# Hybrid decoder trunk, two layers: the state-space scan as one real scan instruction over states turned back by their phase and forward again

## The chip, the cores and the metric

The kernel runs on one core of one Trainium2 chip, in one launch. The metric is the time of a launch in microseconds on the device, as the median of three runs; lower is better. Engines are named as in the profile: PE (matrix products), DVE (VectorE), ACT (ScalarE), POOL (GpSimd), SP (which issues the DMAs).

## The reference

Two layers, 512 tokens, width 1024, all in float32. What matters here is the state-space group of each layer (S5): 32 channel groups of 16 channels drive 64 complex states each.

```python
lam = lax.complex(lam_re, lam_im)
a_bar = jnp.exp(lam * dt)
b_bar = ((a_bar - 1.0) / lam)[..., None] * b_mat
bu = jnp.einsum('bsgc,gpc->bsgp', ug.astype(jnp.complex64), b_bar)
a_elems = jnp.broadcast_to(a_bar, bu.shape)
_, states = lax.associative_scan(combine, (a_elems, bu), axis=1)   # x[s] = a_bar x[s-1] + bu[s]
y = jnp.einsum('bsgp,gcp->bsgc', states, c_mat).real.reshape(B, S, SSM_WIDTH)
```

Beside it, on the same normed input, stands an attention group of 8 heads (causal softmax in query blocks of 128). Both are normed, projected together, and added to the hidden state; then come cross-attention into 256 memory tokens and a SwiGLU feed-forward block.

## The kernel before, in words

Each matrix product is three: operands are split into a high part (ACT, L209, L238, L241) and a low part (DVE or POOL, L210, L239, L242), and `mm3` (L213) issues three matmuls. A block of weights (128x1024) is loaded by `load_w` (L203); the low parts of the memory projection's weights (`xkv`, L943) are POOL's, its result tiles in the PSUM tag `f`, which has one bank, are evicted by DVE at L959.

Tokens of the state-space group are taken eight at a time (T = 8), so that 512 tokens make 64 columns j. `s5_params` (L403) makes, once per layer, the powers of a_bar and from them the matrices by which PE turns eight inputs into a state (`s5_v`, L775), a state into eight outputs (`s5_y`, L881), and inputs into outputs directly (`s5_y0`, L864). What is left between `s5_v` and `s5_y` is the recurrence over the 64 columns with the complex factor A = a_bar^8, for 2048 states (128 partitions x 16). `s5_scan` (L800) does it in two levels: the columns as 8 x 8, seven inner steps (pieces 0 to 2, `step` at L810, six DVE instructions each on 128 to 256 elements, strided), six outer steps over the eight block ends `Sj` (piece 3, on 16 to 32 elements), and a join (pieces 4 and 5), which adds A^i times the carried state to every inner state, its real half on DVE and its imaginary half on POOL (L846 to L851). Eight DMAs (L854) bring the result into the layout `W` that `s5_y` multiplies with. Large tiles of this part share the tag `s5b`, six slots of 128x2048.

The order: attention goes in units (head, pair of query blocks), and a table `PLAN` (L164) says after which unit each part of the other work is emitted: "x" memory projection, "v" `s5_v`, "m" `s5_y0`, "c" a piece of `s5_scan`, "y", "G", "g", "s" what follows. The framework then schedules all instructions by priority, against its own timeline, and each engine's queue runs in the order that comes out. Layer 0's parameters are made at the head of the run, layer 1's during the feed-forward block of layer 0 (hook in `ffn`). A softmax (L765) is, on DVE, a reduction (L767), a reciprocal (L769) and a scaling (L773, or on ACT L771), with the exponential on ACT (L768) between.

## Time and profile before

| | |
|---|---|
| Median of 3 runs | 1632.43 us (1628.01 to 1634.59) |
| Span of the profiled execution | 1624.2 us |
| PE busy | 1517.3 us, 93% |
| DVE busy | 975.1 us, 60% |
| ACT busy | 619.6 us, 38% |
| POOL busy | 345.8 us, 21% |

The profiled execution has no time of its own besides its span; the runs' median is 8.2 us above that span. Shares over the whole span are means over stages with different limits, so the stretches in which the state-space scan runs are read by themselves: some 136 to 212 us (layer 0) and 902 to 983 us (layer 1). PEclk in the views is the granted clock of PE, as a share of the upper of its two levels.

### The profile page before, as it was taken

To read this page: it belongs to the slowest core of one execution; us is meant where nothing else is said; L and a number is where in the kernel's file an instruction comes from. 1 tells how busy PE (TensorE), PEld (TensorE's weight loads), DVE (VectorE), ACT (ScalarE), POOL (GpSimd) and SP (SyncE) were. 2 spreads that over 40 slices of the span, in tenths; PEclk is the share of its full clock that TensorE was granted. 3 is DMA by queue.
4 is the path that set the end of the run, shared out by engine and by line. 5 is a ranking of instruction groups with operands and counts; after the bars stand their busy time and mean duration, and the time that the engine had idled before them with its cause. 6 is when DMAs were issued, how large, how long until landed. Compare 5 with 4: busy or idle time off the path is not lost.

```text
span 1624.2 us, 20486 instructions
## 1 busy us (share of the span) xinstructions
PE 1517.3 (93%) x8038; PEld 1272.5 (78%) x8038; DVE 975.1 (60%) x1499; ACT 619.6 (38%) x995; POOL 345.8 (21%) x225
## 2 busy tenths in 40 slices
PE   7779798999999999999998778989999999999997
...
GB/s 224 62 130 105 85 138 135 105 91 42 127 136 99 103 96 99 89 106 91 88 156 155 133 42 146 124 118 93 75 41 92 93 102 99 96 91 105 91 90 75
DMA packets 97488, 169.09 MB, mean 104 GB/s; under 512 B 32496, under 2 KB 55536, under 8 KB 97392
## 3 DMA queue, kind: packets, MB, share of 16 engines
...
HBM read 150.00 MB, written 15.66 MB: 102 GB/s over the span
## 4 chain that ended last, share of the span: by engine, by line
PE 67%; DVE 9%; ACT 4%; DMA 2%; issue 2%; POOL 1%; SPq 1%; DVEq 0%; ACTq 0%; POOLq 0%
PE mm L216 13%; PE mm L218 13%; PE mm L217 12%; PE f L216 7%; PE f L217 7%; PE f L218 7%; ACT whi L209 1%; DVE lo L239 1%; ACT hi L238 1%; DVE s5b L927 1%; DVE wlo L210 1%; DVE sc L818 1%; PE mm L1006 1%; PE mm L1005 1%; DMA s5b<-du 1%
## 5 line engine op out<-in xcount | busy, mean ns | idle before, releaser
L209 ACT ACTIVATE whi<-wraw 128x1024 fp32r<-128x1024 f32 (+1 forms) x234 | 243.3, 1042 | 637.1 <-PE mm L217 312.3
L210 DVE TENSOR_TENSOR wlo<-wraw,whi 128x1024 fp32r<-128x1024 f32 (+2 forms) x196 | 279.4, 1426 | 68.1 <-ACT whi L209 65.9
L216 PE MATMUL mm<-hi,whi 128*128 128x512 f32 x589 | 231.3, 393 | 0.3 <-ACT whi L209 0.3
L218 PE MATMUL mm<-hi,wlo 128*128 128x512 f32 x589 | 230.0, 392 | 0.4 <-DVE wlo L210 0.4
L217 PE MATMUL mm<-lo,whi 128*128 128x512 f32 x589 | 229.7, 391 | 0.0
L1113 POOL TENSOR_TENSOR tmp<-tmp,tmp 128x512 f32<-128x512 f32 x44 | 60.4, 1374 | 573.8 <-DVE tmp L1112 518.9
L216 PE MATMUL mm<-ghi,whi 128*128 128x512 f32 (+1 forms) x368 | 147.1, 400 | 9.3 <-ACT whi L209 7.9
L218 PE MATMUL mm<-ghi,wlo 128*128 128x512 f32 (+1 forms) x368 | 146.5, 398 | 0.4 <-DVE wlo L210 0.4
L217 PE MATMUL mm<-glo,whi 128*128 128x512 f32 (+1 forms) x368 | 146.0, 398 | 0.2 <-DVE glo L239 0.2
L216 PE MATMUL f<-ghi,whi 128*128 128x256 f32 (+2 forms) x432 | 144.2, 334 | 0.0
L218 PE MATMUL f<-ghi,wlo 128*128 128x256 f32 (+2 forms) x432 | 143.0, 331 | 0.8 <-POOL wlo L210 0.8
L217 PE MATMUL f<-glo,whi 128*128 128x256 f32 (+2 forms) x432 | 142.8, 331 | 0.3 <-DVE glo L242 0.3
L216 PEld LDWEIGHTS mm<-hi,whi 128*128 128x128 f32 x589 | 110.9, 188 | 26.2 <-ACT whi L209 2.2
L218 PEld LDWEIGHTS mm<-hi,wlo 128*128 128x128 f32 x589 | 110.7, 188 | 24.5 <-DVE wlo L210 0.8
L217 PEld LDWEIGHTS mm<-lo,whi 128*128 128x128 f32 x589 | 110.8, 188 | 22.9
L210 POOL TENSOR_TENSOR wlo<-wraw,whi 128x1024 fp32r<-128x1024 f32 x38 | 92.0, 2422 | 122.0 <-ACT whi L209 97.2
L216 PE MATMUL f<-hi,whi 128*128 128x512 f32 (+1 forms) x293 | 114.6, 391 | 0.3 <-ACT whi L209 0.3
L218 PE MATMUL f<-hi,wlo 128*128 128x512 f32 (+1 forms) x293 | 114.3, 390 | 0.0
L217 PE MATMUL f<-lo,whi 128*128 128x512 f32 (+1 forms) x293 | 114.2, 390 | 0.0
L964 DVE TENSOR_TENSOR s5b<-mm,s5b 128x512 f32<-128x512 f32 x52 | 35.9, 690 | 108.2 <-PE mm L218 95.9
L238 ACT ACTIVATE hi<-tmp 128x512 fp32r<-128x512 f32 (+1 forms) x100 | 63.0, 630 | 89.4 <-POOL tmp L1113 58.9
L216 PEld LDWEIGHTS f<-ghi,whi 128*128 128x128 f32 (+1 forms) x432 | 83.0, 192 | 8.9 <-issue 0.7
...
## 6 DMA issues: line engine op xcount, KB each, us to landing
...
```

The costliest lines, as they stand in the source:

```text
L209: nc.scalar.activation(hi, raw, AF.Copy)
L210: (eng or nc.vector).tensor_tensor(lo, raw, hi.bitcast(F32), ALU.subtract)
L216: self.nc.tensor.matmul(ps, wh, xh, start=i == 0, stop=False)
L217: self.nc.tensor.matmul(ps, wh, xl, start=False, stop=False)
L218: last = self.nc.tensor.matmul(ps, wl, xh, start=False, stop=i == n - 1)
L238: a = nc.scalar.activation(hi, src, AF.Copy)
L239: b = eng.tensor_tensor(lo, src, hi.bitcast(F32), ALU.subtract)
L818: E0.tensor_tensor(t1[:, ri], src[:, ri], c(Are), ALU.mult)
L927: nc.vector.tensor_tensor(self.so[m].rearrange("p (j s) -> p s j", s=8), yS[:, m], sg.rearrange("p (s j) -> p s j", s=8), ALU.mult)
L964: self.nc.vector.tensor_tensor(self.hs[m], ps, self.hs[m], ALU.add)
L1005: self.nc.tensor.matmul(ps, hi[:, ks], xh, start=False, stop=False)
L1113: nc.gpsimd.tensor_tensor(uf, uf, gf, ALU.mult)
```

## The change

With A = |A| e^(i phi), the state of column j is turned back by j phi. Then the recurrence has the real factor |A| alone, the same for the real and the imaginary part, and one instruction, `tensor_tensor_scan`, runs it along the free dimension: state = factor x state + input. One instruction takes 8 of the 16 state groups at 64 columns, 512 elements; the factor is 0 at each group's column 0, where a new group begins. Afterwards the states are turned forward again. A half of the states (piece 0 or 1) is thus 6 products and sums on 128x8x63, two scans on 128x512 and 6 products and sums on 128x512, all on DVE, in place in `St`, and four DMAs straight from there. The imaginary half of the join on POOL goes, too.

`s5_v` writes columns 1 to 63 directly, and POOL sets column 0 to zero. `s5_params` no longer raises a_bar and A to powers by complex products (36 instructions per layer): angles are multiples, brought into range and put through the sine on ACT (432 elements for the cosine, 432 for the sine), magnitudes by three real products. A table `tab` of cosine and sine of j phi (two 128x1024) is made by ten instructions per layer and stays in an `s5b` slot until the scan is over; `rt` holds the factors. `PLAN` names two pieces "c" where there were six. The rest of the change removes comments.

```diff
...
-CID, CE, CE16, CROPE, NCONST = 0, 128, 256, 272, 276
+CID, CE, CE16, CROPE, CSTEP, NCONST = 0, 128, 256, 272, 276, 285
...
+    const[:, CSTEP:CSTEP + 9] = np.arange(9)
...
-        (-1, "x", 0), (-1, "x", 1), (1, "v", 0), (1, "m", 0), (2, "c", 0), (2, "c", 1), (2, "c", 2), (2, "x", 2),
-        (2, "m", 1), (2, "x", 3), (3, "m", 2), (3, "m", 3), (4, "c", 3), (4, "c", 4), (5, "x", 4), (7, "c", 5),
+        (-1, "x", 0), (-1, "x", 1), (1, "v", 0), (1, "m", 0), (2, "c", 0), (2, "x", 2),
+        (2, "m", 1), (2, "x", 3), (3, "m", 2), (3, "m", 3), (4, "c", 1), (5, "x", 4),
         (7, "y", 0), (8, "y", 1), (8, "y", 2), (9, "y", 3), (13, "G", 0), (13, "g", 0), (14, "x", 5), (14, "g", 1),
         (14, "g", 2), (14, "x", 6), (14, "g", 3), (15, "x", 7), (16, "s", 0),
     ), (
-        (-2, "v", 0), (-2, "c", 0), (-2, "m", 0), (0, "c", 1), (0, "c", 2), (0, "m", 1), (0, "m", 2), (0, "x", 0),
-        (0, "m", 3), (0, "x", 1), (0, "c", 3), (1, "x", 2), (2, "c", 4), (2, "c", 5), (2, "x", 3), (4, "y", 0),
+        (-2, "v", 0), (-2, "c", 0), (-2, "m", 0), (0, "c", 1), (0, "m", 1), (0, "m", 2), (0, "x", 0),
+        (0, "m", 3), (0, "x", 1), (1, "x", 2), (2, "x", 3), (4, "y", 0),
         (5, "y", 1), (6, "y", 2), (6, "y", 3), (6, "x", 4), (11, "G", 0), (12, "x", 5), (14, "g", 0), (14, "g", 1),
         (14, "g", 2), (14, "g", 3), (14, "x", 6), (16, "x", 7), (16, "s", 0),
     ))
...
-        dt, zr, zi, er = sl(), sl(), sl(), sl()
+        dt, zr, er = sl(), sl(), sl()
         P.tensor_tensor(dt, self.econst, ldt, ALU.pow)
         V.tensor_tensor(zr, lre, dt, ALU.mult)
-        V.tensor_tensor(zi, lim, dt, ALU.mult)
         P.tensor_tensor(er, self.econst, zr, ALU.pow)
-        k, r, ab, sn, cs = sl(), sl(), sl(), sl(), sl()
-        self.reduce(zi, k, r)
-        V.scalar_tensor_tensor(ab, r, -1.0, r, ALU.mult, ALU.max)
-        V.tensor_scalar(ab, ab, -1.0, math.pi / 2, ALU.mult, ALU.add)
-        nc.scalar.activation(sn, r, AF.Sin)
-        nc.scalar.activation(cs, ab, AF.Sin)
+
+        z3, k3, mag = sl(3), sl(3), sl(9)
+        V.tensor_tensor(z3[:, 0], lim, dt, ALU.mult)
+        V.tensor_scalar(z3[:, 1], z3[:, 0], float(T), None, ALU.mult)
+        V.tensor_scalar(z3[:, 2], z3[:, 0], float(T * T), None, ALU.mult)
+        self.reduce(z3, k3, z3)
+        slot3 = self.t([128, 2048], "s5b")
+        sn, cs = (slot3[:, 1024 + i * 432:1456 + i * 432].rearrange("p (x t q) -> p x t q", x=3, t=9) for i in range(2))
+        V.tensor_tensor(sn, z3.unsqueeze(2).to_broadcast([128, 3, 9, 16]),
+                        self.c[:, CSTEP:CSTEP + 9].unsqueeze(1).unsqueeze(3).to_broadcast([128, 3, 9, 16]), ALU.mult)
+        self.reduce(sn, cs, sn)
+        V.scalar_tensor_tensor(cs, sn, -1.0, sn, ALU.mult, ALU.max)
+        V.tensor_scalar(cs, cs, -1.0, math.pi / 2, ALU.mult, ALU.add)
+        nc.scalar.activation(sn, sn, AF.Sin)
+        nc.scalar.activation(cs, cs, AF.Sin)
+        V.memset(mag[:, 0], 1.0)
+        V.tensor_copy(mag[:, 1], er)
+        for n in (1, 2, 4):
+            V.tensor_tensor(mag[:, n + 1:2 * n + 1], mag[:, 1:n + 1], mag[:, n:n + 1].to_broadcast([128, n, 16]), ALU.mult)
         slot2 = self.t([128, 2048], "s5b")
         Q = slot2[:, :960].rearrange("p (q w) -> p q w", q=4)
-        pw = slot2[:, 960:1536].rearrange("p (x t q) -> p x t q", x=4, t=9)
-        Pre, Pim, Are, Aim = pw[:, 0], pw[:, 1], pw[:, 2], pw[:, 3]
...
+        pw = slot2[:, 960:1248].rearrange("p (x t q) -> p x t q", x=2, t=9)
+        Pre, Pim = pw[:, 0], pw[:, 1]
+        V.tensor_tensor(Pre, mag, cs[:, 0], ALU.mult)
+        V.tensor_tensor(Pim, mag, sn[:, 0], ALU.mult)
...
-        self.s5A = sa
+
+        self.tab = tab = self.t([128, 2, 16, 8, 8], "s5b")
+        self.rt = rt = self.t([128, 16, 64], "rt")
+        P.memset(rt[:, :, 0:1], 0.0)
+        nc.scalar.activation(rt[:, :, 1:64], mag[:, 8].unsqueeze(2).to_broadcast([128, 16, 63]), AF.Copy)
+
+        def co(x):
+            return x[:, 2, 0:8].rearrange("p t q -> p q t").unsqueeze(3).to_broadcast([128, 16, 8, 8])
+
+        def fi(x):
+            return x[:, 1, 0:8].rearrange("p t q -> p q t").unsqueeze(2).to_broadcast([128, 16, 8, 8])
+        for x, (u, v, op) in enumerate(((cs, sn, ALU.subtract), (sn, cs, ALU.add))):
+            V.tensor_tensor(tab[:, x], co(u), fi(cs), ALU.mult)
+            for hs in (slice(0, 8), slice(8, 16)):
+                w = self.t([128, 8, 8, 8], "tmps")
+                V.tensor_tensor(w, co(v)[:, hs], fi(sn)[:, hs], ALU.mult)
+                V.tensor_tensor(tab[:, x, hs], tab[:, x, hs], w, op)
...
-        X = self.t([128, 2, 16, 8, 8], "s5b")
-        Xf = X.rearrange("p r q a b -> p r q (a b)")
+        self.St = self.t([128, 2, 16, 64], "s5b")
+        nc.gpsimd.memset(self.St[:, :, :, 0:1], 0.0)
...
-                nc.scalar.activation(Xf[:, ri, hf * 8:hf * 8 + 8], pss[ri].rearrange("p (q j) -> p q j", j=64),
-                                     AF.Copy)
-        self.X = X
-
-    def s5_scan(self, l, piece):
...
+                nc.scalar.activation(self.St[:, ri, hf * 8:hf * 8 + 8, 1:],
+                                     pss[ri].rearrange("p (q j) -> p q j", j=64)[:, :, :63], AF.Copy)
+
+    def s5_scan(self, l, hf):
+
+        nc, V = self.nc, self.nc.vector
+        if hf == 0:
+            self.W = self.t([128, 32, 64], "s5b")
+        hs = slice(hf * 8, hf * 8 + 8)
+        c, s = (self.tab[:, x, hs].rearrange("p q a b -> p q (a b)") for x in range(2))
+
+        def turn(n0, to_r, to_i):
+            r, i = (self.St[:, ri, hs, n0:] for ri in range(2))
+            w1, w2 = (self.t([128, 8, 64], "tmps")[:, :, n0:] for _ in range(2))
+            V.tensor_tensor(w1, i, s[:, :, n0:], ALU.mult)
+            V.tensor_tensor(w2, r, s[:, :, n0:], ALU.mult)
+            V.tensor_tensor(r, r, c[:, :, n0:], ALU.mult)
+            V.tensor_tensor(r, r, w1, to_r)
+            V.tensor_tensor(i, i, c[:, :, n0:], ALU.mult)
+            V.tensor_tensor(i, i, w2, to_i)
+        turn(1, ALU.add, ALU.subtract)
+        for ri in range(2):
+            f = self.St[:, ri, hs].rearrange("p q j -> p (q j)")
+            V.tensor_tensor_scan(f, self.rt[:, hs].rearrange("p q j -> p (q j)"), f, 0.0, ALU.mult, ALU.add)
+        turn(0, ALU.subtract, ALU.add)
+        for ri in range(2):
+            for g2 in range(2):
+                nc.sync.dma_start(self.W[ri * 64:ri * 64 + 64].rearrange("p (q g) j -> p q g j", g=2)[:, hs, g2],
+                                  self.St[g2 * 64:g2 * 64 + 64, ri, hs])
```

What the scheduler makes of it, on DVE's queue. First, layer 0, where the scan runs between attention and memory projection. Before (L818 to L822 are the steps, L767 to L773 the softmax, L959 the eviction of a memory tile):

```order
L959 TENSOR_TENSOR s5b_950<-f_1013,mR_340 128x512
L818 TENSOR_TENSOR sc_1337<-s5b_1172,s5A_417 128x128
L819 TENSOR_TENSOR sc_1338<-s5b_1172,nAim_1335 128x128
L767 TENSOR_REDUCE sm_1531<-s_1527 128x1
L821 TENSOR_TENSOR sc_1337<-sc_1337,sc_1338 128x256
L767 TENSOR_REDUCE sm_1531<-s_1529 128x1
L822 TENSOR_TENSOR s5b_1172<-s5b_1172,sc_1337 128x256
L769 RECIPROCAL sm_1531<-sm_1531 128x1
L239 TENSOR_TENSOR lo_1554<-t_1549,hi_1553 128x384
L818 TENSOR_TENSOR sc_1345<-s5b_1172,s5A_417 128x128 x2
L773 TENSOR_SCALAR P_1528<-P_1528,sm_1531 128x384
L819 TENSOR_TENSOR sc_1346<-s5b_1172,nAim_1335 128x128
```

Now (L813 to L818 turn, L822 scans, L924 is the eviction that was L959):

```order
L924 TENSOR_TENSOR s5b_940<-f_941,mR_340 128x512
L813 TENSOR_TENSOR tmps_1327<-s5b_1162,s5b_622 128x8x63
L814 TENSOR_TENSOR tmps_1328<-s5b_1162,s5b_622 128x8x63
L239 TENSOR_TENSOR lo_1281<-t_1275,hi_1280 128x512
L817 TENSOR_TENSOR s5b_1162<-s5b_1162,s5b_622 128x8x63
L239 TENSOR_TENSOR lo_1295<-t_1290,hi_1294 128x384
L815 TENSOR_TENSOR s5b_1162<-s5b_1162,s5b_622 128x8x63
L818 TENSOR_TENSOR s5b_1162<-s5b_1162,tmps_1328 128x8x63
L816 TENSOR_TENSOR s5b_1162<-s5b_1162,tmps_1327 128x8x63
L822 SCALAR_TENSOR_TENSOR s5b_1162<-rt_623,s5b_1162 128x512 x2
L813 TENSOR_TENSOR tmps_1337<-s5b_1162,s5b_622 128x512
L924 TENSOR_TENSOR s5b_940<-f_1003,mR_340 128x512
```

Softmax instructions stood between the steps of the scan; now the first half's turning back, its two scans and the first product of turning forward stand between two evictions, with two low parts (L239) among them.

Second, layer 1, just ahead of its first softmax. Before (the end of the fourth inner step and the fifth, the reduction, the sixth):

```order
L821 TENSOR_TENSOR sc_7536<-sc_7536,sc_7537 128x256
L822 TENSOR_TENSOR s5b_7241<-s5b_7241,sc_7536 128x256
L818 TENSOR_TENSOR sc_7544<-s5b_7241,s5A_4851 128x128 x2
L819 TENSOR_TENSOR sc_7545<-s5b_7241,nAim_7330 128x128
L820 TENSOR_TENSOR sc_7545<-s5b_7241,s5A_4851 128x128
L821 TENSOR_TENSOR sc_7544<-sc_7544,sc_7545 128x256
L822 TENSOR_TENSOR s5b_7241<-s5b_7241,sc_7544 128x256
L767 TENSOR_REDUCE sm_7511<-s_7509 128x1
L818 TENSOR_TENSOR sc_7552<-s5b_7241,s5A_4851 128x128 x2
```

Now (the end of the second half, then the reduction, L770):

```order
L817 TENSOR_TENSOR s5b_7128<-s5b_7128,s5b_4968 128x512
L239 TENSOR_TENSOR lo_7353<-tmp_7027,hi_7352 64x512
L239 TENSOR_TENSOR lo_7357<-tmp_7027,hi_7356 64x512
L815 TENSOR_TENSOR s5b_7128<-s5b_7128,s5b_4968 128x512
L693 TENSOR_TENSOR tmp_7396<-mm_7389,R_7126 128x512
L818 TENSOR_TENSOR s5b_7128<-s5b_7128,tmps_7432 128x512
L239 TENSOR_TENSOR lo_7384<-raw_7381,hi_7383 128x512
L816 TENSOR_TENSOR s5b_7128<-s5b_7128,tmps_7431 128x512
L770 TENSOR_REDUCE sm_7404<-s_7402 128x1
L770 TENSOR_REDUCE sm_7611<-s_7607 128x1
```

The first softmax stood after five of the seven inner steps, with outer steps and join behind it; now it stands behind the whole scan.

Third, layer 0's first softmax on DVE. Before:

```order
L239 TENSOR_TENSOR lo_947<-tmp_750,hi_946 64x512
L690 TENSOR_TENSOR tmp_1111<-mm_1104,R_849 128x512
L239 TENSOR_TENSOR lo_1099<-raw_1096,hi_1098 128x512
L242 SCALAR_TENSOR_TENSOR glo_854<-tmps_851,gn_63,ghi_853 128x256 x2
L242 SCALAR_TENSOR_TENSOR glo_862<-tmps_859,gn_63,ghi_861 128x256
L767 TENSOR_REDUCE sm_1119<-s_1117 128x1
L242 SCALAR_TENSOR_TENSOR glo_862<-tmps_859,gn_63,ghi_861 128x256
L767 TENSOR_REDUCE sm_1140<-s_1136 128x1
```

Now (L557, L554 and L558 make the table `tab`):

```order
L557 TENSOR_TENSOR tmps_627<-s5b_372 128x512
L557 TENSOR_TENSOR tmps_630<-s5b_372 128x512
L557 TENSOR_TENSOR tmps_634<-s5b_372 128x512
L554 TENSOR_TENSOR s5b_622<-s5b_372 128x1024 x2
L239 TENSOR_TENSOR lo_1089<-raw_1086,hi_1088 128x512
L540 SCALAR_TENSOR_TENSOR s5b_389<-const_85,gn_63,s5b_389 128x16 x4
L558 TENSOR_TENSOR s5b_622<-s5b_622,tmps_627 128x512
L558 TENSOR_TENSOR s5b_622<-s5b_622,tmps_630 128x512
L770 TENSOR_REDUCE sm_1109<-s_1107 128x1
L558 TENSOR_TENSOR s5b_622<-s5b_622,tmps_634 128x512
```

The table's instructions came in ahead of the first reduction, and the split of the memory columns (L242) moved behind it.

## Rows read from the trace of the kernel before

**Rows 1.** Page, part 1: engine, busy us, share of the span, instructions.

```profile
PE 1517.3 (93%) x8038; PEld 1272.5 (78%) x8038; DVE 975.1 (60%) x1499; ACT 619.6 (38%) x995; POOL 345.8 (21%) x225
```

**Rows 2.** Busy time by stretch: from:to, length, each engine's busy us (count), clock, DMA, GB/s.

```profile
118.00:136.00 18.00, 13.53 (x158) 12.55 (x159) 3.40 (x8) 6.02 (x11) 5.78 (x4) 0.81 0.58 101
136.00:150.00 14.00, 13.31 (x125) 12.29 (x124) 8.75 (x14) 5.05 (x11) 7.62 (x4) 1.00 0.88 168
150.00:212.00 62.00, 49.68 (x316) 46.12 (x316) 57.49 (x128) 23.39 (x48) 29.24 (x17) 0.81 0.37 76
903.00:933.00 30.00, 23.60 (x143) 21.07 (x142) 29.23 (x50) 15.21 (x24) 10.43 (x7) 0.89 0.51 97
933.00:983.00 50.00, 36.52 (x227) 32.88 (x228) 49.11 (x108) 18.52 (x42) 29.91 (x17) 0.87 0.24 69
```

**Rows 3.** Waits of PE, 150 to 212 us: us in total, times, longest.

```profile
PE f L877 <- DVE s5b L959: 8.0, 2, 6.3
```

**Rows 4.** Timeline of DVE, 180 to 187 us: start, duration, instruction.

```profile
180.22 2.48 DVE L818 TENSOR_TENSOR sc<-Sj,s5A 128x16 f32<-128x16 f32 x2
...
186.42 0.68 DVE L959 TENSOR_TENSOR s5b<-f,mR 128x512 f32<-128x512 f32 x1
```

**Rows 5.** Timeline of POOL, same stretch.

```profile
180.17 2.40 POOL L210 TENSOR_TENSOR wlo<-wraw,whi 128x1024 fp32r<-128x1024 f32 x1 [7.18 <-ACT whi L209]
```

**Rows 6.** Waits of PE, 933 to 983 us.

```profile
PE s L707 <- ACT P L768: 7.4, 3, 5.5
PE mm L737 <- DVE lo L239: 6.2, 2, 4.1
```

**Rows 7.** Busy time by stretch, instructions on tile sc alone.

```profile
136.00:212.00 76.00, 36.62 (x78) 0.84 0.47 93
902.00:983.00 81.00, 34.17 (x78) 0.87 0.34 82
```

**Rows 8.** Groups of DVE, whole span: busy us, mean ns, idle before.

```profile
L849 DVE TENSOR_TENSOR tmps<-nAim,Sj 128x512 f32<-128x512 f32 x4 | 8.1, 2048 | 0.0
...
L850 DVE TENSOR_TENSOR s5b<-s5b,tmps 128x512 f32<-128x512 f32 x4 | 3.1, 822 | 0.0
```

**Rows 9.** Groups of POOL, 136 to 212 us.

```profile
L210 POOL TENSOR_TENSOR wlo<-wraw,whi 128x1024 fp32r<-128x1024 f32 x8 | 19.2, 2400 | 24.2 <-ACT whi L209 24.2
...
L850 POOL TENSOR_TENSOR s5b<-s5b,tmps 128x512 f32<-128x512 f32 x2 | 3.6, 1822 | 0.0
...
L851 POOL TENSOR_TENSOR s5b<-s5b,s5b 128x448 f32<-128x448 f32 x2 | 2.7, 1368 | 0.0
```

**Rows 10.** Groups of DVE by shape, 98 to 240 us.

```profile
L895 DVE TENSOR_TENSOR s5b<-s5b,f 128x512 f32<-128x512 f32 x4 | 2.7, 683 | 0.8 <-PE f L892 0.8
...
L511 DVE TENSOR_TENSOR s5b<-s5b,tmps 128x512 f32<-128x512 f32 x2 | 2.3, 1168 | 0.0
```

**Rows 11.** Groups of DVE, whole span: the parameter ladder.

```profile
L442 DVE TENSOR_TENSOR s5b<-s5b 128x16 f32<-128x16 f32 (+2 forms) x12 | 3.7, 305 | 0.1
...
L445 DVE TENSOR_TENSOR s5b<-s5b 128x16 f32<-128x16 f32 (+2 forms) x12 | 2.3, 188 | 0.1
```

**Rows 12.** Timeline of DVE, 98 to 137 us.

```profile
110.89 0.29 DVE L767 TENSOR_REDUCE sm<-s 128x1 f32<-128x128 f32 x1 [0.46 <-PE s L710]
...
124.87 1.68 DVE L242 SCALAR_TENSOR_TENSOR glo<-tmps,gn,ghi 128x256 fp32r<-128x256 f32 x4 [6.22 <-ACT ghi L241]
134.06 0.69 DVE L959 TENSOR_TENSOR s5b<-f,mR 128x512 f32<-128x512 f32 x1 [7.51 <-PE f L218]
```

**Rows 13.** Timeline of DVE, 896 to 936 us.

```profile
902.23 1.57 DVE L818 TENSOR_TENSOR sc<-s5b,s5A 128x128 f32<-128x128 f32 x1 [0.86 <-ACT s5b L796]
...
932.70 0.62 DVE L822 TENSOR_TENSOR s5b<-s5b,sc 128x256 f32<-128x256 f32 x1
933.23 0.28 DVE L767 TENSOR_REDUCE sm<-s 128x1 f32<-128x128 f32 x1
```

More of the change, by code (lines that the diff above doesn't have):

```diff
@@ L145 @@
     BUFS = {"raw": 3, "whi": 2, "wlo": 2, "wraw": 2, "hi": 17, "lo": 17, "ghi": 4, "glo": 4, "tmp": 5, "tmps": 3, "R": 4, "s5b": 6, "P": 4,
[L146 removed]
+            "mm": 2, "f": 1, "s": 3, "t": 2, "sm": 8, "stat": 4}
     XKV_POOL = tuple(range(16))
     GLU_POOL, MG_POOL, QK_POOL, ROPE_POOL, MST_POOL = 1, 0, 1, 0, 1
[L151 removed]
     POOLQ = ((1, 3), (0, 1, 2, 3))
@@ L430, in s5_params @@
+        for n in (1, 2, 4):
+            V.tensor_tensor(mag[:, n + 1:2 * n + 1], mag[:, 1:n + 1], mag[:, n:n + 1].to_broadcast([128, n, 16]), ALU.mult)
         slot2 = self.t([128, 2048], "s5b")
         Q = slot2[:, :960].rearrange("p (q w) -> p q w", q=4)
-        pw = slot2[:, 960:1536].rearrange("p (x t q) -> p x t q", x=4, t=9)
-        Pre, Pim, Are, Aim = pw[:, 0], pw[:, 1], pw[:, 2], pw[:, 3]
-        t1, t2 = sl(4), sl(4)
-        def cmul(ore, oim, are, aim, bre, bim, n):
-            def bc(x):
-                return x.to_broadcast([128, n, 16]) if n > 1 else x
-            a, b = t1[:, :n], t2[:, :n]
-            V.tensor_tensor(a, are, bc(bre), ALU.mult)
-            V.tensor_tensor(b, aim, bc(bim), ALU.mult)
-            V.tensor_tensor(ore, a, b, ALU.subtract)
-            V.tensor_tensor(a, are, bc(bim), ALU.mult)
-            V.tensor_tensor(b, aim, bc(bre), ALU.mult)
-            V.tensor_tensor(oim, a, b, ALU.add)
```

70 lines of the change are left out of this document (removed).

## The prediction

> **What bounds the kernel now.** I read the page first: PE is busy for 93% of the span [rows 1], so only a stretch where PE waits or runs slowly has anything to give. Then busy time by stretch [rows 2]. Between 150 and 212 us (layer 0: attention, memory projection and scan side by side) DVE is busy for 57.49 of 62 us, PE for 49.68, at a granted clock of 0.81 of its upper level (2.4 GHz). Layer 1 repeats it in 903 to 983, DVE 29.23 of 30 and 49.11 of 50. Just before the first one, in 118 to 136, DVE is nearly empty (3.40 of 18). So in two stretches of 62 and 80 us VectorE sets the pace.
>
> PE's waits there say the same. In layer 0 it loses 8.0 us before L877 to an eviction, L959 [rows 3]. Why that eviction is late stands on DVE's timeline: two products of 128x16, L818, took 2.48 us from 180.22 on [rows 4], beside a POOL low-part subtraction of 2.40 us from 180.17 [rows 5], the rest of three steps followed, and L959, queued behind, came at 186.42. In layer 1 PE waits 7.4 us for exponentials and 6.2 for a low part from DVE [rows 6].
>
> **What the change removes.** The complex steps, all that touches their scratch tile `sc`, cost DVE 36.62 us in layer 0 and 34.17 in layer 1 [rows 7]. The join's four DVE groups run from 8.1 down to 3.1 us for both layers (22.0 together) [rows 8], 11 per layer; with some 0.5 for preparing `Sj`, DVE loses 48 us in layer 0 and 46 in layer 1. POOL loses four join groups of 3.6 to 2.7 us in layer 0 (12.6 together; [rows 9] has the first and the last).
>
> **What it adds.** Per layer 24 products and sums of some 512 columns at 0.683 us [rows 10]: 16.4. No row shows the scan instruction, four per layer. Lower bound 0.68, that of one product; upper 1.37, a product and a sum. I take the upper, because each column does both and needs its neighbour's result: 5.5. (The Trainium skill, "DVE: opcode table, instruction layouts, handler registers and perf-mode slots", section 6, says the built-in scan runs at half throughput; by it the sum stays as it is, and no run here shows it yet.) So 22 clean; with blocks by POOL at some 2 us each like that of [rows 4], two in layer 0 and one in layer 1, 26 and 24. Net: DVE loses 22 us in either layer.
>
> **Parameters.** Out go, per layer, six ladder groups, the dearest and cheapest 3.7 and 2.3 for both layers (17.5 together) [rows 11], so 8.7, and small copies worth 2. In come nine instructions on 432 elements at no more than 0.68, about 6, and some fifteen short ones at 0.19 (2.3 for 12) [rows 11], about 3. That is even. New is the phase table, 12 x 512 columns: 8.2 us at 0.68, 14.0 at the 1.17 of a row of that stage [rows 10]; I take 11, as the 1.17 is a mean that has POOL in it. In layer 0 it stands before the first softmax, which was at 110.89 [rows 12]. DVE then idled 6.22 us before 124.87 and 7.51 before 134.06 [rows 12], so most of the 11 fits; I charge **3**. In layer 1 parameters and table are made during the feed-forward stage before, where PE, not DVE, sets the pace: nothing; if that cover were gone, 11. ScalarE's two sines of 432 elements replace two of 16, under the same cover. The eight W transfers are issued as before, straight from the states. In layer 1 four of them now stand on SP's queue ahead of three memory loads, which so wait for the first half of the scan: up to 5 us, kept in the range.
>
> **Layer 0's stretch.** DVE's load in 136 to 212 falls from 66 us (8.75 + 57.49) to 44, so it stops being the limit. PE's 49.68 busy us at clock 0.81 are 40 at the upper level: at most **22** can go. But DVE's queue goes in order. The first half now puts up to ten scan instructions between two evictions of the single `f` bank (L924 in the new file), where short softmax operations stood between steps before. One such tile takes 48 matmuls, 5.1 us at the 13.31 us for 125 of [rows 2]; the DVE work between the evictions is about 9. So some waits stay, and I take half: **11**.
>
> **Layer 1's stretch.** Here the whole scan comes before the first softmax. In the kernel before, five of the seven inner steps lay there too, between 902.23 and 933.23 [rows 13]: 18.6 us of DVE, 26 rows from the first to the last shown. The new scan is 24, so the first softmax comes up to 5 us later and nothing is won until then. After it DVE has 49.11 - (46 - 18.6) = 22 us left to do, and PE's 36.52 at clock 0.87 are 32 at the upper level: 18 of 50 could go, less the 5 and less 5.1 for a tile of 48 matmuls that PE used to do before 933 and now does after the scores: 8. Half again: **4**.
>
> **Sum.** -11 - 4 + 3 = -12 us. The profiled span is 1624.2, the median of three runs 1632.43, 8.2 above it; I take that distance as unchanged, so 1632.4 - 12 = **1620**.
>
> **The rivals.**
> *Full gain.* PE works at its upper level as soon as DVE is free: 22 + 8, table hidden, and up to 7 of PE's 118 to 136 (13.53 at clock 0.81 of 18): -37 at the most, -28 to -37 as a case, about 1600. For it: DVE's new load is below PE's floor in both stretches. Against it: the blocks in DVE's order. Chance 0.19.
>
> *Little change.* The freed time is not on the path, or POOL takes it back. A DVE product of two SBUF inputs stood still for as long as POOL's subtraction lasted [rows 4, 5], and POOL has eight of them, 19.2 us, in layer 0's stretch [rows 9]. All of the 24 new products and sums read two tiles in SBUF and fill most of that stretch's DVE time, so six or seven of the eight would meet one and cost about 1.7 more each: +11 per layer. Half of these 22 on the path, as with the gains, leaves -12 + 11 = -1: 1631. (The Trainium skill, "SBUF — State Buffer", "Who interferes with whom", has this as a rule: DVE and GpSimd share a port pair, held for a whole instruction, and the loser blocks; the trace agrees, with 2.48 us beside 2.40.) Against it: POOL's 12.6 us of join are gone from the same place, which met DVE's half of the join at 2.05 us an instruction. Chance 0.20.
>
> *Slower: blocks of scan ahead of what PE waits for.* Each half is 14 DVE instructions, 12 x 0.68 + 2 x 1.37 = 10.9 us, two halves per layer. If PE has just one tile of 5.1 us to do meanwhile, each costs 5.8, four times 23; the table, not hidden, costs 8 more than the 3. With the forecast's -12 that is -12 + 23 + 8 = +19 in the worst case and +8 with half of the blocks met; I put it between, at 1645. It decides once more than half of the blocks stop PE. Against it: PE has attention tiles of other units in its queue, and in before the same evictions waited behind scan steps as well. Chance 0.15.
>
> *The change doesn't do what it says* (the scan instruction runs far slower than two products): every 1.4 us more per scan adds 11 us over both layers, partly covered; it lies in the two cases above.
>
> **How the numbers follow.** Forecast 0.46, with its own range 1608 to 1629 (a quarter to all but a fifth of the gains, table at 0 to 8); about 0.5%, or 8 us, is what a measurement of this kernel can tell from no change, so 0.36 of it is faster (below 1624) and 0.10 the same. Full gain 0.19, faster. Little change 0.20, the same. Slower 0.15, of which 0.12 lies above 1640.6 and 0.03 the same. Together faster 0.55, same 0.33, slower 0.12. The range 1597 to 1641 leaves out the upper 0.12 and some 0.08 of the full gain below.
>
> **What the new profile would show.** Right: the scan's DVE groups add up to 22 to 26 us per layer with the scan instruction at 1.2 to 1.5; DVE's share in the two stretches down to some 60%; PE's wait for the L924 eviction smaller than 8.0 us; the layer-0 stretch some 11 us shorter, layer 1's some 4. Wrong: scan instructions of 3 us or more; products of 2 us in many places beside POOL; PE idle for 5 us or more before L924's or the softmax's successors; the first softmax of layer 0 later by more than 5 us; a stretch elsewhere (head, feed-forward) that changes by more than 5 us.

## The result, and the profile after

The changed kernel takes **1686.35 us** (median; 1686.11 to 1687.59), the one before 1632.29 in the same comparison: a ratio of 1.034 [1.032, 1.036], **slower** by 54 us (medians) to 56 us (ratio). The forecast of 1620 was wrong, and the range, which ended at 1641, too.

Busy time by engine after, to be held against [rows 1]:

```profile
PE 1562.5 (93%) x8038; PEld 1283.9 (76%) x8038; DVE 953.7 (57%) x1343; ACT 627.2 (37%) x1000; POOL 335.0 (20%) x213
```

DVE lost 21 us net, close to the 22 that the terms of the sum give (48 and 46 off; 26 and 24 for the scan and twice 11 for the table on), though the scan's own term was dearer (below). PE gained 45 us of busy time with the same 8038 matmuls. That is the first surprise: the change touches none of the large products.

Busy time by stretch after (columns as in [rows 2]); the last stretch lies in layer 0's feed-forward block:

```profile
118.00:136.00 18.00, 11.70 (x92) 9.85 (x93) 8.62 (x23) 7.06 (x19) 0.00 (x0) 0.55 0.75 126
136.00:150.00 14.00, 14.00 (x143) 12.70 (x142) 9.85 (x10) 5.56 (x8) 7.32 (x4) 1.00 0.77 116
150.00:212.00 62.00, 50.56 (x319) 45.71 (x320) 42.49 (x73) 25.86 (x55) 23.33 (x13) 0.83 0.49 98
...
650.00:800.00 150.00, 149.80 (x642) 119.84 (x641) 67.00 (x65) 40.14 (x48) 13.85 (x10) 1.00 0.29 95
```

In 150 to 212 DVE came down from 57.49 to 42.49 us, as forecast, and PE made 319 matmuls where it had made 316: nothing was won. In 118 to 136 it made 92 instead of 158. And in 650 to 800, with PE full and the clock at 1.00, it made 642 in 150 us; before made 661 there (row below, in the first group of experiments).

What PE waits for after, first from 118 to 212 us, then from 890 to 1080 us:

```profile
PE t L731 <- DVE P L776: 5.5, 2, 4.1
PE mm L740 <- DVE lo L239: 5.1, 1, 5.1
PE f L842 <- DMA s5b<-dQ: 4.4, 1, 4.4
...
PE mm L216 <- ACT hi L238: 8.3, 1, 8.3
PE f L842 <- DMA raw<-w_uq: 7.2, 1, 7.2
```

The eviction wait of [rows 3], 8.0 us, is gone. In its place stand waits for loads on SP's queue and for DVE, and in layer 1 one for a high part that ACT makes. The last row names w_uq as what ended the wait, but L842 reads only two `s5b` tiles, one of them `m0`, loaded from dQ; e5 below shows which load it is.

Starts on DVE's timeline, in us of the span, of five kernels (e5, e7 and e14 are explained below):

| | before | after | e5 | e7 | e14 |
|---|---|---|---|---|---|
| first softmax, layer 0 | 110.9 | 117.8 | 124.7 | 123.0 | 119.3 |
| first residual sum, layer 0 | 299.5 | 313.9 | 318.1 | 315.9 | 303.2 |
| last residual sum, layer 0 | 840.3 | 871.0 | 862.6 | 860.6 | 848.1 |
| first softmax, layer 1 | 933.2 | 975.8 | 967.6 | 963.9 | 950.0 |
| first residual sum, layer 1 | 1091.0 | 1138.2 | 1132.0 | 1116.5 | 1099.3 |
| last residual sum | 1602.7 | 1662.6 | 1643.8 | 1628.2 | 1611.0 |

Some of the loss lies in each stretch: 14 us up to the first residual, 16 in the rest of layer 0, 12 ahead of layer 1's first softmax, 5 in the block after it, 13 behind it. The first softmax moves by some 7 us between executions of kernels that differ only later, so differences below that in its row mean nothing, and distances between rows say more than the rows. The profiled execution of before was a quick one as well: its span is 1624.2 us, where in the other kernels span and time of one execution differ by 1.8 us (after: 1684.5 and 1686.27), which puts before's median at a span of some 1630. Distances to its column hold up to 6 us too much in all.

### The profile page after: what moved, and what is told of

Same layout as the page of the kernel before. It is cut to its first block, busy times and chain, and to the rows that moved or that the text cites. A ratio compares the mean times of both kernels' runs of the same rounds, so it can differ in the third digit from the quotient of the medians.

```text
span 1684.5 us, 20313 instructions
## 1 busy us (share of the span) xinstructions
PE 1562.5 (93%) x8038; PEld 1283.9 (76%) x8038; DVE 953.7 (57%) x1343; ACT 627.2 (37%) x1000; POOL 335.0 (20%) x213
## 4 chain that ended last, share of the span: by engine, by line
PE 73%; DVE 13%; ACT 5%; DMA 4%; issue 2%; SPq 2%; POOL 1%; DVEq 0%; ACTq 0%; POOLq 0%
PE mm L216 13%; PE mm L218 13%; PE mm L217 13%; PE f L216 7%; PE f L218 7%; PE f L217 7%; DVE lo L239 1%; ACT whi L209 1%; DMA s5b<-dQ 1%; PE f L842 1%; DMA s5b<-du 1%; DVE wlo L210 1%; DVE s5b L822 1%; ACT hi L238 1%; DVE s5b L892 1%
## 5 line engine op out<-in xcount | busy, mean ns | idle before, releaser
L216 PE MATMUL mm<-hi,whi 128*128 128x512 f32 x589 | 235.0, 399 | 0.4 <-ACT whi L209 0.4
L218 PE MATMUL mm<-hi,wlo 128*128 128x512 f32 x589 | 233.8, 398 | 0.4 <-DVE wlo L210 0.4
L217 PE MATMUL mm<-lo,whi 128*128 128x512 f32 x589 | 233.2, 396 | 0.0
L216 PE MATMUL mm<-ghi,whi 128*128 128x512 f32 (+1 forms) x368 | 148.0, 403 | 9.7 <-ACT whi L209 8.3
L216 PE MATMUL f<-ghi,whi 128*128 128x256 f32 (+2 forms) x432 | 147.9, 342 | 1.5 <-ACT s5b L844 1.0
L218 PE MATMUL f<-ghi,wlo 128*128 128x256 f32 (+2 forms) x432 | 146.6, 339 | 0.0
L216 PEld LDWEIGHTS mm<-hi,whi 128*128 128x128 f32 x589 | 111.0, 188 | 29.8 <-ACT whi L209 2.5
L216 PE MATMUL f<-hi,whi 128*128 128x512 f32 (+1 forms) x293 | 116.3, 397 | 0.4 <-ACT whi L209 0.4
L216 PEld LDWEIGHTS f<-ghi,whi 128*128 128x128 f32 (+1 forms) x432 | 85.3, 197 | 11.4 <-ACT s5b L844 1.6
```

The costliest lines, as they stand in the source:

```text
L216: self.nc.tensor.matmul(ps, wh, xh, start=i == 0, stop=False)
L217: self.nc.tensor.matmul(ps, wh, xl, start=False, stop=False)
L218: last = self.nc.tensor.matmul(ps, wl, xh, start=False, stop=i == n - 1)
```

## The experiments

### The place of the operands

The diff widens the tile `const` by nine columns (36 bytes per partition; the allocation grows by 32). Tiles stand in SBUF in the order in which they are first asked for. All that is asked for behind `const`, the operand tiles `hi`, `lo`, `ghi` and `glo` among them, so moved by 32 bytes, while the weights `whi` and `wlo` stand ahead of it and stayed. (No trace prints places; the shifts are worked out from the sizes in the code.) Theory: this distance sets the rate of the large matmuls. The kernel before with nothing but that:

```diff
-CID, CE, CE16, CROPE, NCONST = 0, 128, 256, 272, 276
+CID, CE, CE16, CROPE, NCONST = 0, 128, 256, 272, 285
```

**e1_before_shift32.** 

> The kernel before, with nine unused columns at the end of the table const (276 to 285), so that every tile placed behind it in SBUF, the operand slots hi, lo, ghi and glo among them, starts 32 bytes further on; the order of all instructions is the same. Theory A (place of the operands): the changed kernel's matmuls of 128x512 have a median of 396 ns where before they had 389, with the granted clock at 1.00 in both, and it loses 15 us between 491 and 810 us, in a stage that the change does not touch; if it is the shift of the operands, this kernel shows 396 ns too and takes 30 to 45 us more than before, about 1662 to 1677. Rival B (the changed order of the scan, or what DVE and POOL do): 389 ns and 1632 us.

**e2_before_shift64** (292 columns). 

> The kernel before with sixteen unused columns in const (276 to 292): the same tiles are 64 bytes further on. A with the remainder of the address by 64 as what counts: 389 ns and 1632 us, as before. A with a longer period (128 or more): a median other than 389. B: 1632.

**e3_after_shift64** (the kernel after, 296 columns). 

> The changed kernel with const padded from 285 to 296 columns: operand slots 64 bytes behind their place in the kernel before, the order of all instructions as in the changed kernel. A: medians back at 389 ns, and some 30 to 45 us of the 54 us are gone, about 1642 to 1656. B: 396 ns and 1686.

**e4_before_all_shift32** moves weights and operands together:

```diff
+        nc.gpsimd.memset(self.t([128, 8], "pad"), 0.0)
```

as the first tile of all. 

> The kernel before with a tile of 32 bytes placed ahead of all others, so that weights (whi, wlo) and moving operands (hi, lo, ghi, glo) all move by 32 bytes. If the place of the moving operand alone counts: 396 ns and 1662 to 1677, as the first. If it counts that weights and moving operand lie alike: 389 ns and 1632. B: 1632.

**e5_after_old_places** is the kernel after, with the nine columns in a tile of their own that stands behind the operands:

```diff
+        if l == 0:
+            self.step = self.t([128, 9], "step")
+            nc.sync.dma_start(self.step, self.A["const"][:, CSTEP:CSTEP + 9])
```

> The changed kernel with its nine step columns in a small tile of their own, placed behind hi, lo, ghi and glo, so that const is 276 wide again and these tiles lie exactly where they lie in the kernel before; the order of the instructions is the changed kernel's. The two tiles' places cost 24 us (shift of 32) and 8 us (shift of 64) in the kernel before, and a shift of 64 instead of 32 gave back 19 in the changed one. If place and schedule add up: medians of 389 ns and 1686 - 24 to 27, about 1659 to 1662; what is left above 1632, some 28 us, is the changed schedule's. Rival (the place alone): 1632. Rival (the place costs the changed kernel no more than the 19 seen): 1667.

**e6_before_shift96** (300 columns). 

> The kernel before with const 300 wide: moving operands 96 bytes further on, weights in place. If the distance between weights and moving operands counts by its remainder by 128, with 0 best (389 ns), 64 next (392) and 32 worst (396): 96 is like 32, since it is 32 short of 128, about 1656. If it counts by the remainder by 64: as the shift of 32, 1656, too; if each further 32 bytes costs its own amount: another value, between 1640 and 1670.

**e12_after_shift128** (the kernel after, 308 columns). 

> The changed kernel with const 308 wide: operands 128 bytes behind their place in the kernel before, weights in place, the order as in the changed kernel. If the distance between weights and operands counts by its remainder by 128: as e5 (old places), about 1660 to 1664, median 389 ns. If the distance has a longer period or the old place was special: 1667 or more, as with 64, median 392 ns or more.

Measured, with the matmuls counted in 650 to 800 us (PE full, clock 1.00 in each):

| operands moved against weights | kernel | time, us | ratio to before | matmuls |
|---|---|---|---|---|
| 0 | before | 1632 | 1 | 661 |
| 0 (both by 32) | e4 | 1626.93 | 0.997 [0.994, 0.999] | 660 |
| 0 | e5 (after) | 1662.20 | 1.017 [1.014, 1.020] | 661 |
| 32 | e1 | 1655.99 | 1.014 [1.011, 1.017] | 642 |
| 32 | after | 1686.35 | 1.034 [1.032, 1.036] | 642 |
| 64 | e2 | 1639.63 | 1.004 [1.002, 1.006] | 654 |
| 64 | e3 (after) | 1667.63 | 1.022 [1.020, 1.024] | 654 |
| 96 | e6 | 1657.83 | 1.015 [1.013, 1.018] | 642 |
| 128 | e12 (after) | 1681.88 | 1.030 [1.029, 1.032] | 645 |

Several expectations missed in size: a shift of 32 costs before 24 us and not 30 to 45 (e1), one of 64 is not free (e2, e3), and one of 128 is not back at the start (e12).

The row of that stretch in the kernel before, and in e1:

```profile
650.00:800.00 150.00, 149.83 (x661) 123.50 (x660) 68.90 (x67) 40.50 (x48) 13.82 (x10) 1.00 0.30 95
```

```profile
650.00:800.00 150.00, 149.81 (x642) 119.86 (x641) 67.82 (x66) 39.77 (x48) 13.74 (x10) 1.00 0.27 92
```

150 us by 661 is 227 ns a matmul, by 642 it is 234. The instruction view of line L216 (least, median and greatest ns) says the same of one kind; first before, then e1:

```profile
L216 PE MATMUL mm<-hi,whi x589: 387/389/767, 13.9 to 1596.4; 128*128 128x512 f32 x196, 128*64 128x512 f32 x1
```

```profile
L216 PE MATMUL mm<-hi,whi x589: 390/396/628, 13.5 to 1627.9; 128*128 128x512 f32 x196, 128*64 128x512 f32 x1
```

A stretch that the change doesn't touch runs 3% slower, in e1 as in after, at the same instructions and the same clock; with the operands back in place (e5) the rate is back, and with weights and operands moved together (e4) it never leaves. e1 moves other tiles, too, so a control is needed: matmuls with both operands behind `const`. Their group (mean ns) is the same, first before, then e1:

```profile
L218 PE MATMUL mm<-hi,lo 128*128 128x512 f32 x45 | 19.8, 440 | 0.0
```

```profile
L218 PE MATMUL mm<-hi,lo 128*128 128x512 f32 x45 | 19.8, 440 | 0.0
```

Their mean has stretches at the lower clock in it; the median of all 64 products of `hi` and `lo` at 128x512 is 397 ns in before, e1, e2 and e6 alike, while that of the 1034 of `hi` and `wlo` is 389, 396, 392 and 399. So it is the distance between weights and operands that decides, not a tile's own address, as far as one common shift of 32 (e4) shows. It costs before 1.4% and after 1.034 - 1.017 = 1.8%, some **29 us**. e12 rules out that only the distance within 128 bytes counts. Which of the two streams waits, and why, no run tells.

### W's transfers on SP's queue

In before the pieces with the join issue W's DMAs, and `PLAN` has them late (layer 1: two units later than the scan's steps). In layer 0 W so stands on SP's queue behind the second load for `s5_y0` (before: L872 is that load, L854 is W; SPq is SP's DMA queue):

```profile
171.82 3.85 SPq L872 DMA_DIRECT2D s5b<-dQ  x8
...
206.65 4.14 SPq L854 DMA_DIRECT2D s5b<-s5b  x6
```

In after W's DMAs are issued straight from the states, right behind each half of the scan. SP's timeline of e5 in layer 1 (L829 is W, L840 the loads for `s5_y0`):

```profile
930.27 2.73 SPq L829 DMA_DIRECT2D s5b<-s5b  x4
...
935.41 5.26 SPq L840 DMA_DIRECT2D s5b<-dQ  x8
...
959.64 3.76 SPq L840 DMA_DIRECT2D s5b<-dQ  x8
```

PE's timeline of the same kernel, at what it waits for:

```profile
931.61 1.22 PE L216 MATMUL mm<-hi,hi 128*128 128x512 f32 x2 [8.45 <-ACT hi L238]
...
947.77 3.65 PE L845 MATMUL f<-s5b,s5b 128*128 128x64 f32 x16 [7.84 <-DMA raw<-w_uq]
...
971.46 3.64 PE L845 MATMUL f<-s5b,s5b 128*128 128x64 f32 x16 [6.78 <-issue]
```

SP issues W at 930.27, when the first half is done; the loads for the memory, `w_uq` and `s5_y0` stand behind it. The wait of 7.84 us is one for the first load for `s5_y0`: by the trace its last piece landed at 947.68, just ahead of L845, and the w_uq that the profile names at 948.08, behind it. W also takes an `s5b` slot that early, and the second load for `s5_y0` comes only at 959.64, after a wait for PE's L845 to free a slot (its last piece landed at 971.05, and L845 started at 971.46):

```profile
SPq L840 <- PE f L845: 11.9, 1, 11.9
```

**e7_w_apart** makes W's tile and DMAs a part "d" of its own, in layer 1 where the join ended, in layer 0 right behind each half, as e5 has it:

```diff
-        (0, "m", 3), (0, "x", 1), (1, "x", 2), (2, "x", 3), (4, "y", 0),
+        (0, "m", 3), (0, "x", 1), (1, "x", 2), (2, "d", 0), (2, "d", 1), (2, "x", 3), (4, "y", 0),
```

> The kernel of e5 (changed schedule, old places) with the W transfers of a half taken out of the scan's piece: in layer 1 they are a part of their own, emitted where the pieces of the old join were; in layer 0 they follow the scan as now. In layer 1 of e5 PE waited 7.8 and 6.8 us before the direct products of L845, whose table m0 (from dQ) is loaded on SP's queue behind four W transfers that wait for the first half of the scan, and 8.5 us before L216 for a high part that ACT makes behind an eviction which stands behind that half on DVE. Theory (SP's queue and the slot that the phase table holds): m0 is loaded some 20 us earlier, the first two waits go, and 8 to 15 us of e5's 1662 are gone: 1647 to 1654. Rival (DVE's blocks alone delay layer 1): the waits move to DVE, 1658 to 1664.

Measured: 1648.29 us, 1.010 [1.008, 1.011]; the intervals of e5 and e7 don't meet, and 0.0072 is **12 us**. From layer 1's first softmax to its first residual sum it takes 152.6 us where e5 took 164.4. PE's waits of 7.84 and 6.78 us for the two loads are gone: the first load is issued from 896.95 us on, 38 us earlier than in e5, the second some 28 earlier:

```profile
931.10 1.94 SPq L843 DMA_DIRECT2D s5b<-dQ  x4
...
937.55 2.90 SPq L843 DMA_DIRECT2D s5b<-dQ  x4
```

The wait for ACT fell, too (8.45 us in e5, 2.4 in e7). The framework made other orders for PE and DVE in this stretch from the moved part, so the 12 us belong to the move with all that came of it.

**e14_w_apart_both** does the same in layer 0, with "d" behind the seventh unit, where the join had ended:

```diff
-        ... (2, "c", 0), (2, "d", 0), (2, "x", 2),
+        ... (2, "c", 0), (2, "x", 2),
-        (2, "m", 1), (2, "x", 3), (3, "m", 2), (3, "m", 3), (4, "c", 1), (4, "d", 1), (5, "x", 4),
+        (2, "m", 1), (2, "x", 3), (3, "m", 2), (3, "m", 3), (4, "c", 1), (5, "x", 4), (7, "d", 0), (7, "d", 1),
```

> The kernel of e7 (after, operands at the places of before, W's transfers in layer 1 at the old place of the join), with W's transfers of layer 0, too, as a part of their own behind the last memory tile but two, and the phase table where the change has it. Theory (in layer 0 the second memory tile's load waits on SP's queue behind W, 4.0 us for PE): 1643 to 1646. Rival (layer 0's loads wait for their slot in s5b, not for the queue): the 1648 of e7, within 2 us.

Measured: **1633.46 us, 1.001 [1.000, 1.002]**: 0.0086, or 14 us, below e7, where the theory had said 2 to 5. SP's timeline of e7 (L832 is W, L843 the load for `s5_y0`), then of e14:

```profile
183.96 5.48 SPq L832 DMA_DIRECT2D s5b<-s5b  x8
...
192.34 3.77 SPq L843 DMA_DIRECT2D s5b<-dQ  x8
```

```profile
183.46 3.77 SPq L843 DMA_DIRECT2D s5b<-dQ  x8
...
210.65 5.54 SPq L832 DMA_DIRECT2D s5b<-s5b  x8
```

The load comes 8.9 us earlier. W itself had not waited for the scan here: in e7 it stood 6.1 us for a slot that PE's L848 freed, and the load 2.0 us behind W's transfers. So slot and queue both made the load late. In e7 PE waited 4.0 us for it, in e14 not at all; but more than that hung on it. Busy time by stretch in e7, then in e14:

```profile
150.00:212.00 62.00, 51.26 (x332) 46.37 (x331) 43.85 (x71) 23.96 (x51) 23.65 (x13) 0.84 0.52 104
197.00:212.00 15.00, 10.99 (x56) 9.87 (x55) 4.71 (x12) 5.15 (x12) 3.41 (x3) 0.66 0.63 106
```

```profile
150.00:212.00 62.00, 56.40 (x402) 51.75 (x401) 47.57 (x76) 28.34 (x59) 26.33 (x15) 0.92 0.44 90
197.00:212.00 15.00, 15.00 (x118) 14.16 (x118) 6.87 (x15) 8.13 (x16) 5.12 (x4) 1.00 0.15 51
```

In the 15 us from 197 on PE was busy for 10.99 at a mean clock of 0.66 in e7, for all 15 at the upper level in e14, and made 118 matmuls instead of 56. So a stretch at a lower clock went with the wait of 4 us: in e7 PE stood still until 203.82, and the granted clock is 1.00 from 194 to 200 us, 0.65 from there to 206 and 0.50, the lower level, to 212. Here, too, the orders of DVE and PE in layer 0's stretch changed with the move. Of the 14 us, the rows place 9 between layer 0's first softmax and its first residual sum (192.9 to 183.9 us) and 3 in layer 1's block (152.6 to 149.3); the rest lies ahead of the first softmax, within its spread.

### Is DVE's time in the two stretches worth anything?

**e13_before_no_join**: the kernel before without outer steps and join, with no table, no scan instruction and no tile moved.

```diff
-                self.Wt = self.t([128, 2, 16, 8, 8], "s5b")
...
-            W, Sj, hs = self.Wt, self.Sj, slice(hf * 8, hf * 8 + 8)
+            W, hs = X, slice(hf * 8, hf * 8 + 8)
...
-            outer()
+            pass
```

> The kernel before, with the outer steps and the join left out in both layers: W goes out straight from the inner steps' states, in the places where the join stood, so the carrying of states from block to block is not computed. DVE loses its seven outer steps and half of the join, some 20 us per layer, POOL its half, 13 us per layer; all tiles ahead of the operands keep their places, there is no table and no scan instruction. Theory (the premise of the forecast: in the two stretches DVE's time is on the path): the time falls by 12 to 25 us, to 1607 to 1620, most of it in the two stretches, half or so of the 40 us taken away. Rival (the freed DVE time is hidden behind the transfers, POOL's splits and PE's clock): 1628 or more. Between 1620 and 1628 the premise holds for one layer only, and the milestones tell which.

Measured: 1608.45 us, 0.987 [0.984, 0.989]. The page shows DVE at 937.2 us and POOL at 323.3: 38 and 22 less than [rows 1]. So 60 us of work taken off two engines gave 22 us. In the profiled executions the gain lies in the two blocks: from first softmax to first residual sum it takes 179.4 us instead of 188.6 in layer 0 and 151.1 instead of 157.8 in layer 1. In its two stretches:

```profile
150.00:212.00 62.00, 55.12 (x398) 52.69 (x398) 48.89 (x105) 29.93 (x66) 22.24 (x12) 0.92 0.48 111
933.00:983.00 50.00, 50.00 (x376) 47.95 (x374) 32.11 (x75) 25.53 (x56) 23.27 (x13) 0.95 0.42 113
```

PE makes 398 matmuls in the first (e14: 402) instead of 316, and 376 instead of 227 in the second [rows 2], though the second window starts 8 us later by the kernel's own time. The premise holds in the main: the work of DVE and POOL there is on the path. How much of the 22 us is DVE's is open: POOL's part is in it, a slot of `s5b` (the join's result) came free, and W went out earlier. But W stays behind both loads, where `PLAN` has it, with no join to wait for (L860 is the load, L842 is W):

```profile
175.84 1.90 SPq L860 DMA_DIRECT2D s5b<-dQ  x4
193.25 5.49 SPq L842 DMA_DIRECT2D s5b<-s5b  x8
```

### The table and the scan

**e8_no_table_layer0**: e5 with layer 0's table left out (zeros from POOL, so the scan there turns by nothing meaningful).

```diff
+        if l == 0:
+            P.memset(tab, 0.0)
+            return
```

> The kernel of e5 with layer 0's phase table left out (ten DVE instructions; POOL sets the tile to zero instead, so the states of layer 0 come out as zero). In e5 PE waits 5.7 us for L501, 6.0 for a low part and 4.1 for a scaled P between 106 and 129 us, 16 in all where before it waited some 5, and the first softmax is 7 to 14 us later than before. Theory (the table fills DVE's queue where layer 0's parameters and first softmax are due): 5 to 10 us less, 1652 to 1657. Rival (it fits into DVE's idle time behind, as forecast: 3 us or less): 1659 to 1662.

Measured: 1655.95 us, 1.015 [1.013, 1.016] against e5's [1.014, 1.020]. The intervals overlap, and with the change's other waits still in place this told nothing. **e15_w_apart_both_no_table0** is the same edit made on e14. 

> The kernel of e14 with layer 0's phase table left out (one fill with zeros on POOL in its place; layer 0's scan so works on numbers of no meaning, its instructions stay). Theory (the table ahead of the first softmax delays it by more than the 3 us charged): 5 to 10 us below e14. Rival (the table is hidden in DVE's idle time, and the first softmax is late for another reason): within 2 us of e14. The forecast's 3 us lies between.

Measured: 1627.87 us, 0.997 [0.996, 0.999], which is 0.0035, or **5.7 us**, below e14; the intervals don't meet. The first softmax came 5.3 us earlier, which by itself is within its spread. Where the table was charged, in 118 to 136 us, first e14 and then e15:

```profile
118.00:136.00 18.00, 11.81 (x85) 9.56 (x85) 10.18 (x27) 7.01 (x18) 0.00 (x0) 0.50 0.85 133
```

```profile
118.00:136.00 18.00, 12.83 (x126) 11.56 (x126) 3.81 (x9) 4.85 (x10) 1.49 (x1) 0.68 0.77 154
```

**e9_no_recurrence**: e5 with each scan instruction replaced by one product of the same size, so that states aren't carried from column to column.

```diff
-            V.tensor_tensor_scan(f, self.rt[:, hs].rearrange("p q j -> p (q j)"), f, 0.0, ALU.mult, ALU.add)
+            V.tensor_tensor(f, f, self.rt[:, hs].rearrange("p q j -> p (q j)"), ALU.mult)
```

> The kernel of e5 with each of the eight scan instructions replaced by a product of the same size (the recurrence is left out); the order of all instructions stays. The scan took 2.0 us where 1.37 was forecast, a product takes 0.68: DVE has 8 x 1.3 = 10 us less to do. Theory (DVE's time there is hardly on the path any more; queues and places cost the time): 0 to 3 us less, 1659 to 1662. Rival (the scan instruction's length is what makes the change slower): 8 us or more, below 1654.

Measured: 1652.66 us, 1.013 [1.012, 1.015]. The interval meets e5's, so the 0.0034, or 5.5 us, is not clear of noise. From the first softmax to the last residual sum the profiled execution took 1510.8 us instead of 1519.1: 3.4 less up to layer 0's first residual sum, 2.6 ahead of layer 1's first softmax, 2.3 in the block behind it. So eight scans cost some 5 to 10 us over eight products (9.5 by the medians): more than the theory's 0 to 3, and near to the rival, whose 1654 the median is just below. The groups of DVE in after, all of the scan and the table (busy us, mean ns, idle before):

```profile
L822 DVE TENSOR_TENSOR_SCAN s5b<-rt,s5b 128x512 f32<-128x512 f32 x8 | 15.9, 2016 | 0.0
L557 DVE TENSOR_TENSOR tmps<-s5b 128x512 f32<-128x512 f32 x8 | 9.1, 1151 | 3.5 <-POOL s5b L498 3.5
...
L554 DVE TENSOR_TENSOR s5b<-s5b 128x1024 f32<-128x1024 f32 x4 | 7.5, 1922 | 3.1 <-PE s L534 3.1
...
L558 DVE TENSOR_TENSOR s5b<-s5b,tmps 128x512 f32<-128x512 f32 x8 | 5.3, 678 | 0.0
```

The scan's mean is 2016 ns. DVE's timeline in layer 0, then POOL's, shows of what it is made:

```profile
146.78 4.53 DVE L822 TENSOR_TENSOR_SCAN s5b<-rt,s5b 128x512 f32<-128x512 f32 x2
...
166.25 1.20 DVE L822 TENSOR_TENSOR_SCAN s5b<-rt,s5b 128x512 f32<-128x512 f32 x1
...
168.68 3.40 DVE L822 TENSOR_TENSOR_SCAN s5b<-rt,s5b 128x512 f32<-128x512 f32 x1
```

```profile
146.65 2.47 POOL L210 TENSOR_TENSOR wlo<-wraw,whi 128x1024 fp32r<-128x1024 f32 x1 [4.36 <-ACT whi L209]
...
166.42 2.12 POOL L239 TENSOR_TENSOR lo<-tmp,hi 128x512 fp32r<-128x512 f32 x1 [2.54 <-ACT hi L238]
168.51 2.50 POOL L210 TENSOR_TENSOR wlo<-wraw,whi 128x1024 fp32r<-128x1024 f32 x1
```

The scan at 166.25 takes 1.20 us, though a POOL subtraction begins 0.17 us behind it. The one at 168.68 begins 0.17 us behind a subtraction of 2.50 us and takes 3.40, about the subtraction's rest and its own time. So it goes for all eight: three began just behind a subtraction and took 3.3 to 3.4 us, the other five 1.19 to 1.21.

### Repairs taken together

**e10_repaired**: e14, with layer 0's table also held back, as a part "T" that must follow the first unit's softmax:

```diff
+        (-1, "x", 0), (-1, "x", 1), (0, "T", 0), (1, "v", 0), (1, "m", 0), (2, "c", 0), (2, "x", 2),
...
+            self.after(V.tensor_tensor(tab[:, x], co(u), fi(cs), ALU.mult), dep)
```

> The changed scan with three repairs: old places of the operands (e5), W transfers as a part of their own in both layers (e7, now in layer 0, too, where PE still waited 4.0 us for the second m0), and layer 0's phase table held behind the last softmax reciprocal of the first attention unit (e8 showed 6 us for it, leaving it out). If the three add up: 1648 - 6 - 4 = 1638, with waits for L501 and for P below 2 us at 105 to 130 us. Rival (the table only blocks later, in the scan's stretch): 1645 to 1650.

Measured: 1639.34 us, 1.005 [1.003, 1.007], so 0.004 worse than e14 with the table in the way. PE's waits in its layer 0, 118 to 215 us:

```profile
PE f L855 <- DMA s5b<-dQ: 12.9, 2, 11.7
PE s L805 <- DMA dCA<-s5b: 6.8, 1, 6.8
```

The first softmax came at 112.9, but the sines then hold an `s5b` slot until the table is made, and a load for `s5_y0` waits for the last product of the table (L567). PE waits 11.7 us for that load. SP's queue, 118 to 160 us:

```profile
SPq L850 <- DVE tmps L567: 6.8, 1, 6.8
```

The table's place was moved, its price not removed. That the forecast of 1638 came out is luck: W's place in layer 0, priced at 4, was worth 14 (e14), and the new wait hid that.

**e11_repaired_front** adds e4's tile ahead of all to e10. 

> The kernel of e10 with 32 bytes ahead of all tiles, as in e4, where weights and operands keep their distance and the kernel before gained 5 us. Theory (the distance alone counts, e4's 5 us are of the size of the spread): the same as e10 within 5 us. Rival (the place itself counts, too): 5 us less than e10.

Measured: 1642.44 us, 1.006 [1.003, 1.008]: as e10. So e4's 0.3% is not to be had here. e4 remains the only version with nothing left out that was below both kernels, by 5 us.

## Why the prediction was wrong

By ratios: after 1.0343, e5 1.0167, e7 1.0095, e14 1.0009. Of the 56 us, 29 are the operands' place, 12 are W's transfers in layer 1, 14 those in layer 0, and 1.5 is all that the scan, the table and the saved steps come to. Added up this way each step holds for its order of repair. The 1.5 is a balance: between before and e14 the milestones move by +8 us up to the first softmax, -5 in layer 0's block, +4 in the rest of layer 0, +9 ahead of layer 1's first softmax and -8 in its block (together more than 1.5, as before's profiled execution was a quick one).

- **A step that was missing.** The tile's nine columns were not costed at all, though the diff shows them: 29 us. Under "What the new profile would show" the prediction did name the sign by which it shows, a feed-forward stretch that changes by more than 5 us.
- **"The eight W transfers are issued as before, straight from the states."** This is the step that failed by working. That they moved up on SP's queue was said of layer 1 alone, of three memory loads, at up to 5 us, and kept out of the sum. Measured: 12 us there, with the second `s5_y0` load among the late ones for want of a slot, and 14 in layer 0, where the text saw nothing. What kept W late in before was the place of its pieces in `PLAN`, not the join's work (e13): the change put the transfers into the scan's pieces and so moved them.
- **Layer 0's stretch, -11.** The mechanism was right and the size wrong. DVE's load fell as forecast (57.49 to 42.49 us), and in e14 PE makes 402 matmuls in 150 to 212, not 316; but from first softmax to first residual sum that is 188.6 to 183.9 us, so -5. PE still waits there 4.2 us for DVE, for a low part that stands behind a scan of 3.40 us and a product of 2.82: the rival with the blocks, at a small size.
- **Layer 1's stretch, -4.** From the last residual sum of layer 0 to the first softmax e14 needs 101.9 us, before 92.9 (the four kernels with before's order 90.8 to 94.3): +9, where the forecast had up to 5. Then 149.3 instead of 157.8: -8.5, where it had 8 and took half. Net nothing.
- **Layer 1's parameters and table, charged at nothing.** The cover by PE's work was not whole. From layer 0's first residual sum to its last it takes 544.6 to 545.1 us in e5, e7, e9, e14 and e15, and 540.8 in before; in e14 PE waits once, in the matmuls that transpose the parameters' matrices (L512), for DVE. Before has no single wait above 1.9 us there.

```profile
PE s L512 <- DVE s5b L501: 3.9, 1, 3.9
```

- **The scan at 1.37 us.** 1.20 where no subtraction of POOL had begun ahead of it, 2.02 in the mean. (The Trainium skill, "DVE: opcode table, instruction layouts, handler registers and perf-mode slots", section 6, says that the built-in scan runs at half throughput; 1.20 beside 0.68 for a product, 1.76 times, is near that.) The bound above, 1.37, held for the instruction and not for its company: POOL's subtractions, which the text did count for products, met three of the eight scans. DVE's scan work came to 56 us for both layers, with 50 forecast.
- **The table, 11 us on DVE and 3 charged.** On DVE 9.1 + 7.5 + 5.3 = 22 for both layers, so 11: right. On the path 5.7, not 3 (e15). Why is argued, from the order: the softmax reductions stand behind the table, and the idle time of [rows 12] comes later.
- **The rivals.** "Little change" (0.20) has the number that the change itself gives, once its two side effects are repaired (e14), but not the reason: the freed time is on the path (e13), and what it gives in the two blocks goes on the table, the parameters and the scan ahead of the softmaxes. "Slower" (0.15) had the right sign and the wrong mechanism: not blocks of scan, but loads behind transfers and slower matmuls.
